# Twenty input panels of a gated decoder block by seven half-size block products, with the mixer branches moved behind them

## The chip, the cores and the metric

The kernel runs on one core of a Trainium2 chip. The metric is the device time of one execution in microseconds (us). 

## The reference, cut to what matters

One layer of a decoder with three parallel token mixers, for 1024 prompt tokens and 64 sample tokens (8 sequences of 8), D = 1024. All 1088 tokens share all weights.

```python
h = rmsnorm(x, norm_g) * (1 + scale) + shift            # scale, shift, gate from silu(c) @ w_mod
(mg, u, va, za, q, k, vb, ob, zb, ig, fg, p, zc) = split(h @ w_in)
va = layernorm(gelu(va));  ya = gelu(u) * chunk_spatial_gate(va) * silu(za)        # branch A
hb = mlstm(q, k, vb, ig, fg, C0, n0, m0)                                           # branch B, chunks of 128
yb = head_layernorm(sigmoid(ob) * hb) * silu(zb)
yc = (multiscale_pool(p) @ w_pool) * pool_scale * silu(zc)                         # branch C
g_a, g_b, g_c = split(sigmoid(mg))
x = x + gate * ((g_a * (ya @ w_br_a) + g_b * (yb @ w_br_b) + g_c * (yc @ w_br_c)) @ w_out)
y = rmsnorm(x, final_norm_g)
```

`h @ w_in` is 1088 x 1024 by 1024 x 13320. All values are fp32; the outputs are y, the new mLSTM states, the pooling rows and the normalised va of the samples.

## The kernel before, in words

**Panels.** Every large product is cut into weight panels of 1024 x 256: 52 of the input projection, 12 of the three branch projections, 4 of the output projection. fp32 is made of two fp32r parts: a high part (a cast on ScalarE, ACT) and a low part (the rest, a subtraction on VectorE, DVE), so each product is three matmuls on TensorE (PE): high by high, high by low, low by high. `Stream` loads a panel in quarters from the SP queue (`raw`) and splits them (L75 the cast, L78 the subtraction), one panel ahead of its use. The activations h stand split in 16 tiles of 128 features by 1088 tokens (`hhi`, `hlo`).

**Two forms of a panel.** `b_panel` (L194) gives [feature, token]: two feature tiles by three token groups of 364, 362 and 362 columns are six *units*, each of 8 x 3 matmuls into one PSUM bank; there are eight banks. After a unit comes its evacuation, some splitting of the next panel, and one `tick`. `a_panel` (L227) gives [token, feature]: nine units of 256 columns. With `kouter` a `b_panel` goes over the eight k tiles outside and holds six banks to its end.

**Side work.** `self.side` is a list of generators; `tick` runs the first one to its next `yield`, so the work of the mixers is strewn between the units in the order of the program. There is no scheduler: each engine executes its instructions in the order in which they are written.

**The order of the program.** `start` makes h and does panels q0, q1, q2; then q3, va (4 `a_panel`), k (4), v (4 `a_panel`), ob (4 `a_panel`), p and zc in turn (8), zb (4), u and za in turn (8), mg (12), the branch projections (12), the output projection (4). Beside k, v and ob run `gen_ln` and `gen_sgu` (branch A: normalise va, mix positions into `sd`), `gen_gates` (rows of the mLSTM gates) and `gen_gate` (the third part of adaLN, tiles `wg`, `wgs`). `gen_pool` (branch C) of a group g starts behind panel p,g. `gen_prompt` and `gen_sample` (branch B) start with zb and run beside zb, u, za and mg, one step a unit.

**The steps of `gen_prompt`**, ten for each chunk of 128 tokens: scores q k (L1179), times the decay E (L1181), split into P (L139, L140); an empty step; two heads, two heads (L1194 with the split state `Cs` and the weighted q `qs`, L1196 with P; evacuated by L1197 to L1199 into t, st and den); k transposed and weighted into `ks` (L1208, L1213, L1214); the state's update for two heads (L1228, evacuated into C by L1230); split of these two into `Cs`, the other two heads, and the start of `lstm_tail` (short operations on `lsm`, a power on GpSimd); split of the other two and the norm of t (L1098); the next chunk's decays (rb, E) and the split of its v into `vs`; `lstm_out` (L1110 transposes t, L1111 makes yb) and the next chunk's qw, split into `qs`. `gen_sample` has some twelve steps of preparation and end, and 32 steps of one sequence and head each: four products with the split state (L1381), two for the update (L1386), the split of the next state, two updates of C (L1391). With each new head eight masked k tiles `km` are made (L1351).

## Time and profile before

| what | value |
|---|---|
| three runs | 1881.25, 1882.26, 1882.21 us; median 1882.21 us |
| profiled execution: span, first to last instruction | 1883.7 us (no other time of it is given) |
| TensorE busy | 1856.6 us, 99% of the span |
| VectorE busy | 871.6 us, 46% |
| ScalarE busy | 555.7 us, 30% |
| GpSimd busy | 212.8 us, 11% |
| matmuls | 12473 |
| bytes moved by DMA | 234.37 MB, 124 GB/s in the mean |

A row of the groups gives line, engine, operation, out<-in by the names of the program, shapes and count, then busy us and mean ns of one, then the engine's idle time just ahead and what ended it. Matmuls overlap, so the time of one in a stream is the length of a stretch of the chain of waits, divided by its matmuls, and not the mean ns of the group. Rows in order of time give start and length in us; idle time ahead stands in square brackets with what ended it.

### The profile page before, as it was taken

What the parts mean: (1) busy time and instruction counts of PE and PEld (TensorE: products, weight loads), DVE (VectorE), ACT (ScalarE), POOL (GpSimd) and SP (SyncE); (2) the same over time, 40 slices, a digit from 0 to 9 for tenths busy, and PEclk for the clock granted to TensorE, in tenths of its full rate; (3) what the DMA queues carried; (4) which work ended last, traced back from release to release, by engine and by line L of the source; (5) the groups of instructions that cost most, each with busy time, mean ns of one, the idle gap of its engine ahead of it and who ended that gap; (6) DMA issues with size and microseconds to landing.
All of it is one profiled execution on the core that took longest, in us unless ns stands there. A gap on an engine that the chain in (4) does not pass through costs nothing.

```text
span 1883.7 us, 30152 instructions
## 1 busy us (share of the span) xinstructions
PE 1856.6 (99%) x12473; PEld 1845.0 (98%) x12473; DVE 871.6 (46%) x1638; ACT 555.7 (30%) x1108; POOL 212.8 (11%) x340
## 2 busy tenths in 40 slices
PE   7999999999999999999999999999999999999998
PEld 7899999999999999999999999999999999999998
DVE  7751125424321445536566666444443324374444
ACT  5352222113332222223333333343222312121223
POOL 3440000011100000000000000021221000000023
PEclk8889999999999999999999999999999999999999
DMA  6233122333432212154353444255555434372422
GB/s 248 96 106 103 41 84 93 99 123 100 151 99 84 65 60 71 59 177 135 118 154 102 148 149 147 82 159 170 184 191 166 172 117 163 108 248 90 153 68 96
DMA packets 155228, 234.37 MB, mean 124 GB/s; under 512 B 16145, under 2 KB 122321, under 8 KB 155091
## 3 DMA queue, kind: packets, MB, share of 16 engines
q1 hardware_dynamic: 137490, 168.33, 28.9%
q0 software_dynamic: 17456, 63.85, 9.4%
q8 instruction: 98, 1.61, 0.3%
q14 instruction: 40, 0.32, 0.1%
q10 hardware_dynamic: 144, 0.26, 0.0%
HBM read 164.10 MB, written 68.30 MB: 123 GB/s over the span
## 4 chain that ended last, share of the span: by engine, by line
PE 94%; DVE 2%; ACT 0%; issue 0%; DMA 0%; POOL 0%; POOLq 0%; SPq 0%; ACTq 0%; DVEq 0%
PE ps L194 63%; PE ps L227 19%; PE ps L233 2%; PE ps L953 1%; PE ps L1228 1%; PE ps L1194 1%; PE ps L456 1%; PE ps L1381 1%; PE ps L1179 1%; PE ps L761 1%; PE ps L1196 1%; PE ps L1110 0%; PE ps L623 0%; PE ps L1386 0%; PE ps L1208 0%
## 5 line engine op out<-in xcount | busy, mean ns | idle before, releaser
L194 PE MATMUL ps<-hhi,whi 128*128 128x362 f32 (+1 forms) x1824 | 602.8, 331 | 0.0
L194 PE MATMUL ps<-hhi,wlo 128*128 128x362 f32 (+1 forms) x1824 | 599.4, 329 | 0.0
L194 PE MATMUL ps<-hlo,whi 128*128 128x362 f32 (+1 forms) x1824 | 599.0, 328 | 0.0
L78 DVE TENSOR_TENSOR wlo<-raw,whi 128x512 fp32r<-128x512 f32 (+1 forms) x272 | 186.2, 700 | 357.3 <-ACT whi L75 357.1
L194 PEld LDWEIGHTS ps<-hhi,whi 128*128 128x128 f32 x1824 | 344.4, 189 | 0.6 <-ACT mg L1028 0.4
L194 PEld LDWEIGHTS ps<-hlo,whi 128*128 128x128 f32 x1824 | 344.7, 189 | 0.0
L194 PEld LDWEIGHTS ps<-hhi,wlo 128*128 128x128 f32 x1824 | 343.6, 188 | 0.0
L227 PE MATMUL ps<-whi,hhi 128*128 128x256 f32 (+1 forms) x768 | 219.3, 286 | 0.0
L227 PE MATMUL ps<-wlo,hhi 128*128 128x256 f32 (+1 forms) x768 | 215.6, 281 | 0.0
L227 PE MATMUL ps<-whi,hlo 128*128 128x256 f32 (+1 forms) x768 | 215.6, 281 | 0.0
L75 ACT CAST whi<-raw 128x512 fp32r<-128x512 f32 (+1 forms) x272 | 161.1, 616 | 108.5 <-PE ps L194 105.4
L194 PE MATMUL ps<-yhi,whi 128*128 128x362 f32 (+1 forms) x576 | 189.3, 329 | 0.0
L194 PE MATMUL ps<-yhi,wlo 128*128 128x362 f32 (+1 forms) x576 | 189.0, 328 | 0.0
L194 PE MATMUL ps<-ylo,whi 128*128 128x362 f32 (+1 forms) x576 | 188.9, 328 | 0.0
L227 PEld LDWEIGHTS ps<-whi,hhi 128*128 128x128 f32 x768 | 144.7, 188 | 0.8
L227 PEld LDWEIGHTS ps<-wlo,hhi 128*128 128x128 f32 x768 | 145.0, 189 | 0.0
L227 PEld LDWEIGHTS ps<-whi,hlo 128*128 128x128 f32 x768 | 144.8, 189 | 0.0
L194 PEld LDWEIGHTS ps<-ylo,whi 128*128 128x128 f32 x576 | 108.5, 188 | 0.0
L194 PEld LDWEIGHTS ps<-yhi,whi 128*128 128x128 f32 x576 | 108.5, 188 | 0.0
L194 PEld LDWEIGHTS ps<-yhi,wlo 128*128 128x128 f32 x576 | 108.3, 188 | 0.0
L227 PE MATMUL ps<-whi,mhl 128*128 128x256 f32 x512 | 91.5, 281 | 0.0
L1028 ACT ACTIVATE mg<-ps 128x362 f32<-128x362 f32 (+1 forms) x72 | 34.1, 473 | 189.0 <-PE ps L194 185.5
(346 smaller groups left out, 2305.3 us busy)
## 6 DMA issues: line engine op xcount, KB each, us to landing
raw<-in_w_in_dram SPq DMA_DIRECT2D x204, 256.0 KB
mgd<-mg POOLq DMA_DIRECT2D x24, 544.0 KB, 3.0
mgr<-mgd SPq DMA_DIRECT2D x24, 544.0 KB
raw<-in_w_br_dram SPq DMA_DIRECT2D x48, 256.0 KB
yraw<-yd SPq DMA_DIRECT2D x16, 544.0 KB
C<-in_state_C_dram SPq DMA_DIRECT2D x32, 256.0 KB
out_dram<-C POOLq DMA_DIRECT2D x32, 256.0 KB, 3.1
ss<-in_w_mod_dram SPq DMA_DIRECT2D x14, 512.0 KB
```

Source lines behind the costliest of these rows:

```text
L75: kb.A.copy(hi, t[:, :, :n])
L78: kb.V.tensor_tensor(out=p["lo"][:, sl, :n], in0=t[:, :, :n], in1=hi.bitcast(F32), op=ALU.subtract)
L194: self.PE.matmul(ps[:, :n], w[:, k, fs], a[:, g0 : g0 + n], start=(k == 0 and j == 0), stop=(k == nk - 1 and j == 2))
L227: self.PE.matmul(p[:, :cols], a[:, ts], w[:, k, :cols], start=(k == 0 and j == 0), stop=(k == KT - 1 and j == 2))
L233: self.PE.matmul(p[:, :cols], stack[:, k, :], w[:, k, :cols], start=(k == 0 and j == 0), stop=(k == KT - 1 and j == 1))
L456: PE.matmul(sums[-1][u][:, :m], w["hi" if ww else "lo"][:, k, fs], a[:, g0 : g0 + m], start=(k == 0 and part == "high" and j == 0), stop=( ...
L761: PE.matmul(p[:, j * 128 : j * 128 + 128], self.va[b * 4 + j][:, fs], self.w_sguT[:, g, :], start=True, stop=True)
L953: self.PE.matmul(p[:, :n], wsl[:, ww, k, fs], a[:, g0 : g0 + n], start=(k == 0 and j == 0), stop=(k == 1 and j == 2))
L1028: A.activation(st[f][:, g0 : g0 + w], ps, AF.Tanh, scale=0.5)
L1179: PE.matmul(p[:, h * 128 : h * 128 + 128], k[:, 2 * h + d, :], q[:, 2 * h + d, :], start=(d == 0), stop=(d == 1))
L1194: PE.matmul(p[:, :258], qs[x][:, 2 * h + d, :], Cs[d][y][:, h, :], start=(d == 0 and j == 0), stop=False)
L1196: PE.matmul(p[:, :258], P[:, x, h, :], vs[y][:, h, :], start=(c == 0 and j == 0), stop=(j == 2))
```

## The change

**Twenty panels by seven products.** The panels of k, zb, zc, u and za are taken as 2 x 2 blocks: the weight panel by halves of its features and of k, and h by halves of k and of the tokens (544 and 544). With sums of blocks on both sides (Strassen's scheme in Winograd's form) seven products give what eight do. Each is 4 k tiles x 3 matmuls for two groups of 272 columns (`HT`). `Stream.step` makes the seven weight blocks with four sums on VectorE and splits each; `gen_factors` makes the sums of h once and splits them, one of them (`put_t4`) over the upper token half of h's first four k tiles, which is kept in `b12d` and loaded back behind the last of the twenty panels. In `seven` six banks are held as three pairs b1, b2, b5. The first product goes to b1 and is copied to b2, where three more are accumulated; b5 takes two; sums between pairs go over SBUF (x12, x22).

**Order.** q, then the twenty (k, zb, zc, then u and za in turn) with no side work, then va, v, ob, p, mg, the branches and the output. `sd` is gone: gelu(u) times silu(za) is stored as `uzd` by the new stage and multiplied in `gen_sgu`; silu(zc) is stored as `zcd` and loaded in `gen_pool`.

**Pace.** The same generators run beside fewer panels: `gen_ln`, `gen_sgu`, `gen_gates` and `gen_gate` beside v and ob with one tick a unit; `gen_pool` beside p with two; `gen_prompt` and `gen_sample` beside mg with three. What is left is drained before p and before the last mg panel. Panel q3 is now accumulated k outside, while the last factors are made.

The core of the diff:

```diff
+        if p["seven"]:
+            b = lambda q: raw[q][:, :512]
+            if j == 1:
+                p["x"] = self.raw("sum")
+            x = None if p["x"] is None else p["x"][:, :512]
+            if j == 1:
+                V.tensor_tensor(out=x, in0=b(1), in1=b(2), op=ALU.add)
+            elif j == 2:
+                V.tensor_tensor(out=x, in0=x, in1=b(0), op=ALU.subtract)
+            elif j == 4:
+                V.tensor_tensor(out=b(1), in0=b(0), in1=b(1), op=ALU.subtract)
+            elif j == 6:
+                V.tensor_tensor(out=x, in0=b(3), in1=x, op=ALU.subtract)
+            src = x if j in (1, 2, 6) else b((0, 0, 0, 3, 1, 2)[j])
+            self.live -= (0, 0, 0, 0, 2, 1, 2)[j]
...
+        hi, lo = (kb.wsp.tile([128, 528], F32R, tag="u", name=kb.nm(x))[:, :n] for x in ("whi", "wlo"))
+        kb.A.copy(hi, src)
+        self.units += 1
+        p["u"].append((hi, lo))
+        self.pending = (lo, src, hi)
+        if not self.defer:
+            self.flush()
...
-            self.tick()
+            self.tick(self.pace)
...
+    ORDER = (1, 5, 6, 2, 7, 4, 3)
...
+        for i, n in enumerate(self.ORDER):
+            st.need(panel, i + 1)
+            wh, wl = panel["u"][i]
+            bank, new = {1: (b1, True), 5: (b5, True), 6: (b2, False), 2: (b1, False), 7: (b2, False), 4: (b2, False),
+                         3: (b5, False)}[n]
+            for g in range(2):
+                gs = slice(g * HT, g * HT + HT)
+                if self.fresh and n == 1:
+                    PE.matmul(b2[:, g, :HT], wh[:, 0:128], B[1][0][0][:, gs], start=True, stop=True)
+                for j in range(4):
+                    bh, bl = B[n][j]
+                    ks = slice(j * 128, j * 128 + 128)
+                    for m, (w, b) in enumerate(((wh, bh), (wh, bl), (wl, bh))):
+                        PE.matmul(bank[:, g, :HT], w[:, ks], b[:, gs], start=(new and j == 0 and m == 0),
+                                  stop=(j == 3 and m == 2), skip_group_check=True)
+                if n == 7:
+                    copy(view(x22)[:, g, :], b2[:, g, :HT])
+            st.units -= 1
+            if n == 1:
+                self.fresh = False
+                A.copy(cut(b2), cut(b1))
+            elif n == 6:
+                copy(view(x12), cut(b2))
+            elif n == 2:
+                evac(0, 0, cut(b1))
+            elif n == 7:
+                add(view(x22), cut(b5))
+                evac(1, 1, view(x22))
+            elif n == 4:
+                evac(1, 0, cut(b2))
+            elif n == 3:
+                add(view(x12), cut(b5))
+                evac(0, 1, view(x12))
+            for _ in range(2):
+                if st.units < st.UNITS and self.ahead(panel, i) < 6:
+                    st.step()
+            self.tick(self.pace)
...
-        for nm_ in ("q", "va", "k", "v", "ob"):
+        for n in range(4):
+            pan["q", n] = st.add(i["w_in"][self.PANEL["q"] + n])
+        for nm_, n in self.SEVEN:
+            pan[nm_, n] = st.add(i["w_in7"][self.PANEL7[nm_] + n], seven=True)
...
-        self.start()
-        self.inputs_of_mixers()
-        self.pool_branch()
-        self.merge_gates()
-        self.finish()
-
+        tc = self.tc
+        with tc.tile_pool(name="psumA", bufs=8, space=PSUM) as self.psum:
+            self.start()
+        with tc.tile_pool(name="pairs", bufs=1, space=PSUM) as self.pairs:
+            self.seven_panels()
+        with tc.tile_pool(name="psumB", bufs=8, space=PSUM) as self.psum:
+            self.inputs_of_mixers()
+            self.pool_branch()
+            self.merge_gates()
+            self.finish()
...
-        self.side = [finish_rows(0), finish_rows(1)]
+        self.st.used(w1)
+        self.st.defer = True
+        self.side = [finish_rows(0), finish_rows(1), self.gen_factors(0), self.gen_factors(1)]
...
+        self.pace = 2
         self.b_panel(self.pan["q", 2], self.h, self.evac_rows(2, self.qd))
+        self.drain()
+        def hook(k):
+            for j in range(2):
+                if k == j + 1:
+                    self.put_t4(j)
+            if k in (1, 3):
+                self.side = [self.gen_factors(2 + k // 2)]
+            self.tick(2)
+            if k in (5, 6):
+                self.put_t4(k - 3)
+        self.b_panel(self.pan["q", 3], self.h, self.evac_rows(3, self.qd), kouter=True, hook=hook)
+        self.drain()
+        self.pace = 1
...
+        V.tensor_tensor(out=a0, in0=a1, in1=a0, op=ALU.subtract)
+        V.tensor_tensor(out=a1, in0=b1, in1=a1, op=ALU.subtract)
+        V.tensor_tensor(out=b1, in0=b1, in1=a0, op=ALU.subtract)
+        V.tensor_tensor(out=b0, in0=b0, in1=b1, op=ALU.subtract)
+        yield
+        t13 = [self.slot([128, T], F32R, name="t13") for _ in range(2)]
+        self.split(a, *t13)
+        if j % 2 == 0:
+            self.t2[j // 2] = [self.slot([128, T], F32R, name="t2") for _ in range(2)]
+        half = slice((j % 2) * W, (j % 2) * W + W)
+        t2 = [t[:, half] for t in self.t2[j // 2]]
+        self.split(b1, *t2)
+        self.t4[j] = b0
+        lo, up = slice(0, W), slice(W, T)
+        both = lambda t, s: tuple(x[:, s] for x in t)
+        self.B[1][j] = both(self.h[j], lo)
+        self.B[2][j] = both(self.h[j + 4], lo)
+        self.B[3][j] = both(self.h[j + 4], up)
+        self.B[4][j] = both(self.h[j], up)
+        self.B[5][j] = both(t13, lo)
+        self.B[6][j] = tuple(t2)
+        self.B[7][j] = both(t13, up)
...
+    def put_t4(self, j):
+        self.split(self.t4.pop(j), *self.B[4][j])
...
+            self.seven(self.pan[nm_, n], self.B, evac, 0.0625 if nm_ == "k" else None)
+        for j in range(4):
+            for m in range(2):
+                S.dma_start(self.h[j][m][:, W:].bitcast(F32), self.b12d[j, m])
...
-        for n in range(4):
-            self.b_panel(self.pan["k", n], self.h, self.evac_rows(n, self.kd, 0.0625))
...
+            uz = self.slot([128, T], name="uz")
+            self.S.dma_start(uz, self.uzd[f])
...
-                    G.dma_start(self.sd[f], s)
+                    V.tensor_tensor(out=s, in0=s, in1=uz, op=ALU.mult)
+                    G.dma_start(self.yd[0][f], s)
...
+        self.pace = 2
...
+                    S.dma_start(gates[f], self.zcd[2 * g + f])
...
-            self.b_panel(self.pan["zc", g], self.h, evac_z)
...
-            self.b_panel(self.pan["zb", n], self.h, evac_zb)
...
-            self.b_panel(self.pan["u", n], self.h, evac_u)
-            self.b_panel(self.pan["za", n], self.h, evac_za)
-
+        self.pace = 3
...
+                self.drain()
+                self.pace = 1
...
-    nc = bacc.Bacc("TRN2", target_bir_lowering=False, num_devices=1)
+    nc = bacc.Bacc("TRN2", target_bir_lowering=False, num_devices=1, dynamic_dma_scratch_size=8192)
```

Two places in the program's order. In the mLSTM's second chunk, TensorE: the scores (qc, kc) and what follows. TensorE before:

```order
L194 MATMUL ps_8367<-hhi_1113,wlo_8078 128x364
L1179 MATMUL ps_8407<-qc_8087,kc_8088 128x128 x8
L194 MATMUL ps_8420<-hhi_931,whi_8077 128x362
L194 MATMUL ps_8420<-hlo_932,whi_8077 128x362
L194 MATMUL ps_8420<-hhi_931,wlo_8078 128x362
L194 MATMUL ps_8420<-hhi_948,whi_8077 128x362
```

and with the change:

```order
L257 MATMUL ps_11535<-hhi_1131,wlo_11121 128x362
L1391 MATMUL ps_11570<-qc_11369,kc_11370 128x128 x8
L1406 MATMUL ps_11586<-Cs_11396,qs_11531 128x258
L1406 MATMUL ps_11586<-Cs_11397,qs_11531 128x258
L1406 MATMUL ps_11586<-Cs_11396,qs_11532 128x258
L1406 MATMUL ps_11586<-Cs_11398,qs_11531 128x258
L1406 MATMUL ps_11586<-Cs_11399,qs_11531 128x258
L1406 MATMUL ps_11586<-Cs_11398,qs_11532 128x258
L1408 MATMUL ps_11586<-vs_11510,P_11580 128x258 x2
L1408 MATMUL ps_11586<-vs_11511,P_11580 128x258
L1406 MATMUL ps_11599<-Cs_11396,qs_11531 128x258
```

Before, the scores have a unit of panel products on both sides, and the heads come two units later. Now the first head (Cs and qs, then vs and P) follows the scores directly; P is made from these scores.

VectorE at the same place, before (zb is the evacuation of the panel beside, wlo a weight split):

```order
L1153 TENSOR_TENSOR qw_8360<-qc_8087,rb_8091 128x4x128 x2
L140 TENSOR_TENSOR qs_8364<-qw_8360,qs_8363 128x1024
L990 SCALAR_TENSOR_TENSOR zb_8392<-zb_8392,ps_8367 128x364
L78 TENSOR_TENSOR wlo_8396<-raw_8085,whi_8395 128x2x256
L78 TENSOR_TENSOR wlo_8396<-raw_8143,whi_8395 128x2x256
L1181 TENSOR_TENSOR E_8309<-ps_8407,E_8309 128x512
L140 TENSOR_TENSOR P_8417<-E_8309,P_8417 128x512
L990 SCALAR_TENSOR_TENSOR zb_8392<-zb_8392,ps_8420 128x362
L78 TENSOR_TENSOR wlo_8396<-raw_8199,whi_8395 128x2x256
L990 SCALAR_TENSOR_TENSOR zb_8392<-zb_8392,ps_8451 128x362
L78 TENSOR_TENSOR wlo_8396<-raw_8399,whi_8395 128x2x256
L1198 SCALAR_TENSOR_TENSOR t_694_8483<-o_8405,ps_8486 128x256
```

and with the change:

```order
L1365 TENSOR_TENSOR qw_11528<-qc_11369,rb_11373 128x4x128 x2
L203 TENSOR_TENSOR qs_11532<-qw_11528,qs_11531 128x1024
L99 TENSOR_TENSOR wlo_11492<-raw_11123,whi_11491 128x512
L1393 TENSOR_TENSOR E_11505<-ps_11570,E_11505 128x512
L203 TENSOR_TENSOR P_11580<-E_11505,P_11580 128x512
L1410 SCALAR_TENSOR_TENSOR t_1470_11583<-o_11568,ps_11586 128x256
L1411 BN_STATS st_1471_11584<-t_1470_11583 128x6
L1410 SCALAR_TENSOR_TENSOR t_1470_11583<-o_11568,ps_11599 128x256
L1411 BN_STATS st_1471_11584<-t_1470_11583 128x6
L1410 SCALAR_TENSOR_TENSOR t_1470_11583<-o_11568,ps_11639 128x256
L1411 BN_STATS st_1471_11584<-t_1470_11583 128x6
L1410 SCALAR_TENSOR_TENSOR t_1470_11583<-o_11568,ps_11652 128x256
```

The evacuations and most weight splits between the steps of the mLSTM are gone: qs, E, P and the four heads' t and st follow each other.

295 lines of the change are left out of this document (186 added, 109 removed).

## The prediction

> **What bounds the kernel now.** I read the page's busy times first, then the chain of waits, then the stretches, then VectorE's instructions in order of time. The page:
>
> ```profile
> span 1883.7 us, 30152 instructions
> PE 1856.6 (99%) x12473; PEld 1845.0 (98%) x12473; DVE 871.6 (46%) x1638; ACT 555.7 (30%) x1108; POOL 212.8 (11%) x340
> ```
>
> TensorE is busy for 99% of the span, so today a shorter stream of products shortens the kernel, and every wait put before a product lengthens it. The chain of waits, by pieces (start us, us, what), gives the price of a product:
>
> ```profile
> 190.61 22.70 PE ps L227 x192
> 1445.09 331.10 PE ps L194 x1992
> ```
>
> 331.10/1992 is 166.2 ns for a product of 362 or 364 columns (362.7 in the mean), 22.70/192 is 118.2 ns for one of 256. A unit of a feature-major panel, 24 products, is 3.99 us. Stretches (us, then busy time and instructions of PE, PEld, DVE, ACT and POOL, granted clock, DMA share, GB/s):
>
> ```profile
> 80.00:100.00 20.00, 17.09 (x87) 15.65 (x86) 15.79 (x20) 5.12 (x11) 8.96 (x5) 0.74 0.08 24
> 885.00:1440.00 555.00, 554.72 (x3594) 552.37 (x3593) 300.83 (x688) 188.90 (x384) 71.25 (x148) 1.00 0.47 147
> 1445.00:1776.00 331.00, 331.00 (x1994) 330.99 (x1993) 146.75 (x219) 69.69 (x102) 3.07 (x5) 1.00 0.44 147
> ```
>
> In 885 to 1440 the mLSTM generators run beside the panels: VectorE works 300.83 us of 555 and TensorE never waits. That slack is what the change spends.
>
> **What the twenty panels gain.** A panel now has 144 products at 166.2 ns, 23.93 us. By seven block products it has 7 x 2 x 4 x 3 = 168 products of 272 columns. No row has 272 columns; the line through the two rows above has 0.45 ns a column, so 125.4 ns, and 168 of them take 21.07 us. 2.86 us by 20 panels is **57.3 us gained** (50 to 60, if the width costs a little more or less).
>
> Beside them VectorE and ScalarE work more: per panel seven halves instead of four to split, four sums of weight blocks, two sums with b5. By the split's row below (700 ns for 512 columns) VectorE has 11 such, 7.7 us, two sums and up to eight evacuation steps of 544 columns at about 0.75 us, 7.5 us: 15.2 of 21.07 us. ScalarE has seven casts and seven or eight copies at about 0.65 us, some 10 us. Each bank pair is written again only after another product of 3.0 us, which covers copy and sum. I take 2 us for all twenty (0 to 15).
>
> **What is paid before and behind them.** The factors: four times (two sums and one split of 1088 columns at 1.29 us, five operations of 544 at about 0.7 us), 7.4 us each, plus four splits, are 32 us of VectorE, in order, under panels q2 and q3 (48 us) that already hold 3 + 4 us of weight splits and waits on ScalarE. The last factors come late for the first panel's second product, and the six banks of q3, now accumulated together, are emptied only at its end: 6 us (2 to 15). The restore of 2.2 MB from `b12d` has the last product (3.0 us) and four tiles of va (96 products, 11.3 us) as cover: 2 us (0 to 6). The adaLN gate: v and ob have 72 ticks, the four generators need more, so `drain` ends the third and fourth part of `gen_gate` with nothing between:
>
> ```profile
> L140 DVE TENSOR_TENSOR wgs<-wg,wgs 128x1024 fp32r<-128x1024 f32 x8 | 9.8, 1226 | 7.6 <-ACT wgs L139 7.6
> L139 ACT CAST wgs<-wg 128x1024 fp32r<-128x1024 f32 x8 | 8.4, 1044 | 0.0
> ```
>
> One cast and two subtractions are 3.5 us before the one product, the rest behind it mostly hidden by ScalarE running ahead: 5 us (2 to 12).
>
> **The pool branch** had two panels of one step per unit for each group; now it has one panel of two steps, and the last group three.
>
> ```profile
> L78 DVE TENSOR_TENSOR wlo<-raw,whi 128x512 fp32r<-128x512 f32 x268 | 183.4, 700 | 352.3 <-ACT whi L75 352.1
> L140 DVE TENSOR_TENSOR plo<-po,phi 128x1088 fp32r<-128x1088 f32 x8 | 10.3, 1292 | 3.0 <-ACT phi L139 2.7
> L923 DVE TENSOR_TENSOR pa<-pb 128x1039 f32<-128x1039 f32 x8 | 9.9, 1234 | 0.0
> L931 DVE SCALAR_TENSOR_TENSOR po<-pa,pb 128x1008 f32<-128x1008 f32 x8 | 9.6, 1201 | 0.0
> L924 DVE TENSOR_TENSOR psa<-psb 128x176 f32<-128x176 f32 x8 | 2.7, 335 | 0.0
> L139 ACT CAST phi<-po 128x1088 fp32r<-128x1088 f32 x8 | 8.8, 1103 | 2.3 <-DVE po L935 2.2
> ```
>
> Per feature tile a level costs 1.23 + 0.33 us, and 1.20 + 1.10 + 1.29 us follow in a chain. Two tiles with one to four levels, and two weight splits between, are 11.7, 14.8, 17.9 and 21.0 us before the group's first product. It comes after three units (12.0 us), for the last group after two (8.0 us). TensorE waits 0 + 2.8 + 5.9 + 13.0 = 22 us (10 to 35).
>
> **The prompt's mLSTM is the large term.** It takes ten ticks for each of eight chunks, now three to a unit, so a chunk has 3.33 units, 13.3 us, and 84 products of its own of up to 258 columns, at 118.2 ns or less 9.9 us: 23.2 us of TensorE. VectorE executes in order; for one chunk, with what ended each idle time in brackets:
>
> ```profile
> 971.75 1.30 DVE L140 TENSOR_TENSOR Cs<-C,Cs 128x516 fp32r<-128x516 f32 x2
> 972.96 1.66 DVE L1230 SCALAR_TENSOR_TENSOR C<-C,decb,ps 128x258 f32<-128x258 f32 x4
> ...
> 976.99 0.16 DVE L152 SCALAR_TENSOR_TENSOR lsm<-lsm 128x4 f32<-128x4 f32 x1 [1.22 <-POOL lsm L149]
> ...
> 977.58 0.16 DVE L1095 TENSOR_TENSOR lsm<-lsm 128x4 f32<-128x4 f32 x1
> ...
> 978.67 1.29 DVE L140 TENSOR_TENSOR Cs<-C,Cs 128x516 fp32r<-128x516 f32 x2
> 979.89 1.38 DVE L1098 TENSOR_SCALAR t<-t,lmv,lsm 128x256 f32<-128x256 f32 x4
> ...
> 982.84 0.68 DVE L1144 TENSOR_TENSOR rb<-rb,c_maskp 128x512 f32<-128x512 f32 x1
> 985.81 1.23 DVE L140 TENSOR_TENSOR vs<-v,vs 128x1032 fp32r<-128x1032 f32 x1 [2.29 <-ACT vs L139]
> ...
> 988.71 1.28 DVE L1111 TENSOR_TENSOR yb<-ps,c_mnorm_gT 128x512 f32<-128x512 f32 x2
> 989.91 1.28 DVE L1153 TENSOR_TENSOR qw<-qc,rb 128x512 f32<-128x512 f32 x2
> 992.37 1.23 DVE L140 TENSOR_TENSOR qs<-qw,qs 128x1024 fp32r<-128x1024 f32 x1 [1.17 <-ACT qs L139]
> ...
> 994.55 0.68 DVE L1181 TENSOR_TENSOR E<-ps,E 128x512 f32<-128x512 f32 x1
> 995.97 0.69 DVE L140 TENSOR_TENSOR P<-E,P 128x512 fp32r<-128x512 f32 x1 [0.73 <-ACT P L139]
> ...
> 999.52 0.42 DVE L1198 SCALAR_TENSOR_TENSOR t<-o,ps 128x256 f32<-128x256 f32 x1 [0.23 <-ACT den L1197]
> ...
> 1001.04 0.43 DVE L1199 BATCH_NORM_STATS2 st<-t 128x6 f32<-128x256 f32 x1
> ```
>
> Stretch by stretch: 971.75 to 977.74 is 5.99 us; Cs and t, 978.67 to 981.27, 2.60; rb to vs 4.20; yb to qs 4.89; E to P 2.11; two heads 1.95, so four 3.9. The chunk's rest stands some 13 us later:
>
> ```profile
> 1013.27 0.48 DVE L1214 SCALAR_TENSOR_TENSOR ks<-ps,cols,ks 128x256 fp32r<-128x256 f32 x1
> ...
> 1015.70 0.48 DVE L1214 SCALAR_TENSOR_TENSOR ks<-ps,cols,ks 128x256 fp32r<-128x256 f32 x1 [0.54 <-ACT ks L1213]
> ...
> 1017.71 1.66 DVE L1230 SCALAR_TENSOR_TENSOR C<-C,decb,ps 128x258 f32<-128x258 f32 x4
> L139 ACT CAST Cs<-C 128x516 fp32r<-128x516 f32 x60 | 35.9, 621 | 0.0
> ```
>
> ks to ks is 2.91, C 1.66, and the cast ahead of the first Cs 0.62. That is 28.9 us; 2.2 weight splits make 30.4 us, of which 7 us are short waits for ScalarE and GpSimd that nothing fills, since the next instruction stands behind. The chain closes on itself: heads need P and qs, the next chunk's transposes need t. So a chunk cannot follow the last in 23.2 us; it needs 30.4, and more, because three ticks stand together: heads 2 and 3 can stand a unit (4 us) behind 0 and 1, and a cast of Cs stands on ScalarE behind the evacuation of the unit ahead. By walking the three alignments of ten ticks to groups of three I get 2 to 6 us of such idling per chunk and take 4: 34.4 us, **11.2 us more than TensorE needs, 78 us for the seven chunks that have a successor**. Bounds: nothing, if ScalarE and GpSimd come early enough to hide their 7 us; 122 us with 8 us at the borders in all eight.
>
> **The sample mLSTM**: 32 steps, three to a unit.
>
> ```profile
> L1391 DVE SCALAR_TENSOR_TENSOR C<-C,decb,ps 128x258 f32<-128x258 f32 x64 | 27.8, 477 | 0.0
> L1351 DVE TENSOR_SCALAR km<-kst,c_bmask 96x256 fp32r<-96x256 f32 x32 | 9.3, 358 | 0.0
> ```
>
> Each step's products need a split state whose subtraction (0.69 us) stands on VectorE behind the last step's two updates (0.87 us). The first of a group also waits for a cast behind the evacuation (about 1.1 us). A group's 18 products, 2.1 us, then take about 4.1 us: 2.0 us by 10.7 groups is 21 us; the four changes of head, eight km each, add some: 25 us (8 to 50; DMA would set the upper end, some 2 MB for 8 us).
>
> **The sum**, against the profiled span of 1883.7 us: -57.3 + 2 + 6 + 2 + 5 + 22 + 78 + 25 = +82.7, so 1966 us. The median of the runs, 1882.21, is 1.5 us under that span: **1965 us**, slower.
>
> **The rivals.**
> 1. *The waits overlap.* TensorE runs ahead, VectorE never idles; its busy time per chunk then is 30.4 - 7 = 23.4 us, even with TensorE's 23.2. With 5 us for the prompt and the lower ends elsewhere (22) the sum is -30: 1852 us, faster. For it: 300.83 of 555 us. Against: the bracketed waits are there while VectorE has time. It decides once a chunk follows in under about 27 us.
> 2. *The clock falls too.* In 80 to 100 us TensorE idled 2.9 of 20 us and was granted 0.74, against 1.00 where it never idles. About 280 us of products stand in the stages where I expect waits; at 0.85 they take 49 us more, half of it on the path: 1990 us. The Trainium skill, "TensorE: Matmul & The Clock Gate", HAM oscillation, says that an idle stretch beyond about one window of 3.4 us halves the clock until it has been busy again; by that rule waits of 4 to 13 us here would each be followed by slow products. This profile's row agrees in direction.
> 3. *The seven products are not bound by TensorE.* If copies, sums and casts, which wait for each other in order, hold a panel at today's 23.9 us, the 57.3 us are not gained: 2022 us. For it: VectorE at 72%. Against: 3.0 us of cover at each step.
> 4. *The same stalls at half their price*, 70 us: 1895 us.
>
> **How the numbers follow.** Forecast 0.58 (its own range 1925 to 2010); rival 1 0.10, rival 2 0.17, rival 3 0.08, rival 4 0.07, of which 0.03 reach no change or faster. Faster by over 0.2% (about what a measurement of this kernel can tell) 0.11, within it 0.02, slower 0.87. 1900 to 2040 leaves out rival 1 and the far tail.
>
> **What would show it.** Right: 272-column products about 125 ns apart and TensorE near 99% in the seven stage, then, in the mg panels, waits of PE for P, qs, t and Cs on VectorE, a chunk every 34 us, VectorE over 80% there, and four mg panels behind it as before. Wrong: a chunk every 25 us with PE at 99%, or waits inside the seven stage.

## The result and the profile after

The kernel became slower, as forecast, but by much more: **2100.81 us** (2095.85 to 2107.09, four runs) against 1882.24 us (1881.25 to 1885.32, four runs), 1.116 times the time before, 95% interval 1.114 to 1.119. The forecast was 1965 us with a range of 1900 to 2040. The loss is 219 us where 83 us were summed up.

The page of the changed kernel, its first rows and TensorE's granted clock in 40 slices:

```profile
span 2105.3 us, 31462 instructions
PE 1900.0 (90%) x12955; PEld 1854.2 (88%) x12955; DVE 1019.9 (48%) x1814; ACT 617.5 (29%) x1202; POOL 220.7 (10%) x356
...
PEclk8999999999999999999998888888889999999999
```

TensorE's share of the span fell from 99% to 90%. It waits about 205 us, and it is even busy for 43 us longer than before, though its products, at the prices of before, add up to some 57 us less. The clock row shows one reason, a stretch of eights from slice 22 to slice 30. Nothing else became busy. VectorE stands at 48%, ScalarE at 29%.

What TensorE waited for, over the whole run (who waits, whom for; us in total, times, longest):

```profile
PE b L353 <- ACT x L330: 36.7, 32, 3.0
PE ps L1322 <- DVE t L1310: 30.4, 8, 5.6
PE ps L257 <- DVE wlo L99: 22.2, 8, 5.3
PE ps L1212 <- ACT phi L202: 17.6, 4, 8.1
PE ps L1593 <- ACT Cs L202: 10.3, 10, 3.5
PE ps L293 <- DVE wlo L99: 8.8, 5, 6.8
...
PE ps L1593 <- DVE Cs L203: 7.6, 15, 2.5
```

The largest row is one that the forecast had priced at 2 us: line 353 issues the block products, and in 32 places they wait for ScalarE to copy an accumulator out. The second is the prompt's transposes behind VectorE's normalised rows, the fourth the pool's product, the fifth and the last the samples' states. These were foreseen. The third is ordinary units that wait for the low part of their own weights, 13.4 us of it in the prompt; the sum had no such wait.

Stretches of the changed kernel: the seven-product stage, the prompt, the samples, and the merge gates left over (us, then busy time and instructions of PE, PEld, DVE, ACT, POOL, granted clock, DMA share, GB/s):

```profile
172.00:659.00 487.00, 445.68 (x3362) 435.94 (x3362) 213.78 (x330) 162.44 (x296) 17.19 (x33) 0.97 0.26 83
1178.00:1470.00 292.00, 235.74 (x1386) 222.91 (x1384) 171.60 (x415) 89.09 (x199) 23.75 (x44) 0.88 0.40 120
1470.00:1592.00 122.00, 95.77 (x514) 87.61 (x514) 72.62 (x165) 39.89 (x76) 38.14 (x86) 0.86 0.55 182
1592.00:1701.00 109.00, 108.32 (x654) 107.57 (x653) 29.06 (x56) 28.52 (x51) 8.00 (x13) 1.00 0.43 142
```

Twenty panels in 487 us are 24.4 us each; an ordinary panel took 23.93 us. **The seven products saved nothing.** In the prompt and the samples TensorE is granted 0.88 and 0.86 of its clock, so its products take longer there as well as wait. The last row is 4.5 panels of uncovered merge gates at full speed, as the forecast said.

Where the 221.6 us between the two spans went, stage by stage. The measured column is the stage's length less what its products take at the prices of the kernel before (from the starts of successive products in the trace); "slow" is the part that is no gap but products further apart than those prices:

| Term of the sum | forecast | measured | of it slow |
|---|---|---|---|
| twenty panels at 125.4 ns a product | -57.3 | -57 | |
| waits inside the seven products | 2 | 66 | 14 |
| transition to the first block product | 6 | 6 | 1 |
| restore, va, v, ob, gates, gate drain | 2 + 5 | 22 | 5 |
| pool | 22 | 30 | 5 |
| prompt | 78 | 98 | 32 |
| samples | 25 | 46 | 13 |
| merge gates left, and all behind | 0 | 10 | 0 |

### The profile page after: what moved, and what is told of

Read it like the earlier page. It is cut to its first block, busy times and chain, and to the rows that moved or that the text cites. A ratio compares the mean times of both kernels' runs of the same rounds, so it can differ in the third digit from the quotient of the medians.

```text
span 2105.3 us, 31462 instructions
## 1 busy us (share of the span) xinstructions
PE 1900.0 (90%) x12955; PEld 1854.2 (88%) x12955; DVE 1019.9 (48%) x1814; ACT 617.5 (29%) x1202; POOL 220.7 (10%) x356
## 5 line engine op out<-in xcount | busy, mean ns | idle before, releaser
L257 PE MATMUL ps<-hhi,wlo 128*128 128x362 f32 (+1 forms) x864 | 292.0, 338 | 16.5 <-DVE wlo L99 16.5
L257 PE MATMUL ps<-hhi,whi 128*128 128x362 f32 (+1 forms) x864 | 294.0, 340 | 0.0
L257 PE MATMUL ps<-hlo,whi 128*128 128x362 f32 (+1 forms) x864 | 291.1, 337 | 0.0
L353 PE MATMUL b<-t,whi 128*128 128x272 f32 x960 | 190.0, 295 | 31.1 <-ACT x L330 29.1
L353 PE MATMUL b<-hhi,whi 128*128 128x272 f32 x640 | 189.5, 296 | 9.5 <-ACT x L330 7.6
L353 PE MATMUL b<-hlo,whi 128*128 128x272 f32 x640 | 187.4, 293 | 0.0
L353 PE MATMUL b<-hhi,wlo 128*128 128x272 f32 x640 | 186.8, 292 | 0.0
L257 PEld LDWEIGHTS ps<-hhi,wlo 128*128 128x128 f32 x864 | 169.5, 196 | 17.7 <-DVE wlo L99 17.7
L257 PEld LDWEIGHTS ps<-hhi,whi 128*128 128x128 f32 x864 | 170.9, 198 | 0.5 <-PE ps L1527 0.4
L257 PEld LDWEIGHTS ps<-hlo,whi 128*128 128x128 f32 x864 | 170.1, 197 | 0.0
```

Of the source, the lines that this page charges most:

```text
L257: self.PE.matmul(ps[:, :n], part(panel, w, k, fs), a[:, g0 : g0 + n], start=(k == 0 and j == 0), stop=(k == nk - 1 and j == 2))
L353: PE.matmul(bank[:, g, :HT], w[:, ks], b[:, gs], start=(new and j == 0 and m == 0), stop=(j == 3 and m == 2), skip_group_check=True)
```

## The experiments

The lines in the diffs are those of the changed kernel or of the kernel that an experiment starts from. Each is timed beside the kernel before.

### 1. The same order with eight products

Is it the seven products that cost, or the order that they force on the rest? The twenty panels are ordinary ones again, in the same place, with every mixer still behind them:

```diff
-            pan[nm_, n] = st.add(i["w_in7"][self.PANEL7[nm_] + n], seven=True)
+            pan[nm_, n] = st.add(i["w_in"][self.PANEL[nm_] + n])
...
-            self.seven_panels()
+            self.eight_panels()
...
-        self.side = [finish_rows(0), finish_rows(1), self.gen_factors(0), self.gen_factors(1)]
+        self.side = [finish_rows(0), finish_rows(1)]
...
+            self.b_panel(self.pan[nm_, n], self.h, evac)
```

(`eight_panels` is the loop over the twenty panels with the same evacuations; the factors, their copy to `b12d` and the products of q3 for all units at once fall away with the seven products.)

> The twenty panels of k, zb, zc, u and za as ordinary panels of 144 products, at the same place, ahead of the mixers; no factors, q3 ordinary again; all else as in the change. Theory: in the change the stage of the twenty panels takes 483 us, 24.1 us a panel, which is what ordinary panels take (23.9), so the seven products gain nothing and the whole loss comes from the mixers beside fewer panels: 2085 to 2105 us, twenty panels in 478 to 482 us, the prompt's mLSTM still some 36 us a chunk. Rival: the seven products do gain about 57 us and the later stages cost that much more than they seem to: 2140 to 2165 us.

Measured: 2084.55 us (2083.77 to 2085.32), 1.108 times before (1.105 to 1.111), half a microsecond under the theory's range. With ordinary products in the same order the kernel is 16 us *faster* than with seven, and 203 us slower than before. Chunks of the prompt started 32.9, 30.6, 34.5, 44.5, 30.9, 35.2 and 42.2 us apart, as in the changed kernel (32.7, 32.8, 34.8, 45.1, 31.2, 35.2, 42.1). So the price of the order is some 200 us, and beside it the block products, which should have paid 57 us back, cost 16.

### 2. The wait inside the seven products

What the block products wait for is seen best in one panel of zb. ScalarE in order of time (start us, duration, engine, line, operation, in brackets the idle time before it and what ended it):

```profile
280.51 0.62 ACT L130 CAST whi<-sum 128x512 fp32r<-128x512 f32 x1 [2.12 <-DVE sum L119]
281.04 0.38 ACT L330 COPY x<-b 128x272 f32<-128x272 f32 x1
283.39 0.39 ACT L330 COPY x<-b 128x272 f32<-128x272 f32 x1 [1.98 <-PE b L353]
```

and TensorE's two idle places at the same time:

```profile
281.47 0.52 PE L353 MATMUL b<-t,whi 128*128 128x272 f32 x2 [2.23 <-ACT x L330]
...
283.83 0.60 PE L353 MATMUL b<-hhi,whi 128*128 128x272 f32 x1 [0.48 <-ACT x L330]
```

Product 7 lies in two banks of the pair b2, one for each half of the tokens. Behind its first half ScalarE copies that half out (line 330), but ScalarE is in the cast of a weight block, and that cast waited 2.12 us for VectorE's sum of blocks. Until the copy at 281.04 is over, the second half of product 7 does not start, though it writes the other bank: the wait is for the tile, which is the pair (the first kernel below tests this). When the second half is done, product 4 writes the same pair straight away and waits for its copy again. Products 7, 7 and 4 write b2 with nothing between them; each other pair does have another product between.

Two kernels take this away by different means. The first makes b2 two tiles, one for each half, so that only a half's own copy is waited for:

```diff
-        self.b2 = self.pairs.tile([128, 2, 512], F32, tag="b2", name="b2")
+        self.b2 = [self.pairs.tile([128, 512], F32, tag=f"b2{g}", name=f"b2{g}") for g in range(2)]
```

(Copies and evacuations of b2 are then two instructions, one for each half.)

> The change with the pair b2 as two tiles, one for each column group; order and work are the same but that copies and evacuations of b2 are two instructions of 272 columns. Theory: the second half of product 7 and the first half of product 4 wait because ScalarE's copy of one half is held against the other half of the pair as well; with two tiles the 0.77 us waits go and the 2.5 us waits shrink to about 1 us: the stage falls from 483 to 435 to 455 us, the kernel to 2050 to 2075 us. Rival: the waits come from ScalarE being late behind casts that wait for the weight sums; then the stage stays above 470 us.

Measured: 2057.08 us (2055.84 to 2058.32), 1.093 times before (1.090 to 1.096).

The second keeps the pair, gives product 3 a pair of its own, and lays product 3 between 7 and 4; x22 is then copied once for both halves:

```diff
-    ORDER = (1, 5, 6, 2, 7, 4, 3)
+    ORDER = (1, 5, 6, 2, 7, 3, 4)
...
+        b3 = self.pairs.tile([128, 2, 512], F32, tag="b3", name=self.nm("b3"))
...
-                         3: (b5, False)}[n]
+                         3: (b3, True)}[n]
...
-                if n == 7:
-                    copy(view(x22)[:, g, :], b2[:, g, :HT])
...
             elif n == 7:
+                copy(view(x22), cut(b2))
+                add(view(x12), cut(b5))
                 add(view(x22), cut(b5))
```

(The weight blocks are made in the new order, too.)

> The change with product 3 in a pair of its own (b3, the two free banks), done between products 7 and 4, and one copy of b2 behind product 7: a product of 3.0 us now stands between the copy of b2 and the next write to it, as between all other pairs; VectorE has one sum of 544 columns more per panel. Theory: the 51 us of gaps in the stage go nearly all, and the 13 us of slow products behind them: the stage takes 422 to 432 us, the kernel 2040 to 2055 us. Rival (late ScalarE, or VectorE at its limit): gaps move to the next product and the stage stays above 450 us.

Measured: 2054.13 us (2050.96 to 2057.3), 1.092 times before (1.087 to 1.096). The same stretch, of the kernel with two tiles and then of the one with its own pair for product 3:

```profile
174.00:611.00 437.00, 426.54 (x3361) 423.88 (x3360) 212.74 (x340) 168.14 (x354) 16.39 (x32) 1.00 0.28 92
```

```profile
174.00:611.00 437.00, 426.80 (x3362) 425.93 (x3362) 228.59 (x352) 161.53 (x283) 17.32 (x33) 0.99 0.29 93
```

The stage lasts 437 us in both, 50 less than in the changed kernel, and the remaining waits for copies are, in the first and in the second kernel:

```profile
PE b L353 <- ACT x L330: 10.2, 11, 1.5
```

```profile
PE b L354 <- ACT b L359: 7.0, 3, 2.4
```

The first are those of product 4 for its own half, the second those of product 6 for the copy from b1 to b2. Both kernels fall in the range of their theory, though the stage of the second was expected to take 422 to 432 us.

426.80/3362 is 126.9 ns for a product of 272 columns where the forecast took 125.4, and 437/20 is 21.8 us a panel where it took 21.07: the price of the block products was right, and the wait was what hid it. Against the same order with eight products (2084.55 us) the second kernel gains 30 us: 42 in this stage, where twenty ordinary panels of 23.93 us take 479, less what stands around it. With the gaps the clock came back too, from 0.97 to 0.99 and 1.00; of the 14 us of slow products in this stage 4 are left. The one with its own pair for product 3 is the base of the runs that follow, 2054 us.

### 3. Two steps behind a unit, not three

The mixers' steps follow a unit of 24 products three at a time. With two for the pool's last group and the prompt there is more dense work beside each chunk:

```diff
-        self.side += [self.gen_prompt(), self.gen_sample()]
-        self.pace = 3
+        self.side += [self.gen_prompt(), self.faster(), self.gen_sample()]
+        self.pace = 2
```

`faster` sets the pace to 3 once the prompt is done. The kernel is otherwise the changed one.

> The change with two ticks a unit beside the mg panels until the prompt's mLSTM is done, then three. A chunk has five units instead of 3.33, so TensorE alone needs 29.5 us a chunk. Theory: a chunk is held by VectorE's chain of 30 us and the idling at group borders, so a chunk follows in 32 to 36 us as before, and 1.67 units a chunk, 53 us, of the panels behind are done in that time: 2035 to 2060 us. Rival: each group has its own price and more groups cost more; a chunk takes 40 us or more and the kernel stays within 15 us of the change's 2101 us.

Measured: 2072.21 us (2070.78 to 2073.64), 1.101 times before (1.098 to 1.105): 29 us won of the changed kernel's loss. Chunks were 38.7, 37.4, 40.0, 40.7, 38.1, 38.8 and 43.2 us apart, so neither theory held: more dense products, less idle time (48 us in the prompt against 66), but chunks 3 us *longer*. The chunk did not keep its length, as the theory had it, and the kernel did not stay where it was, as the rival had it. The next guess is that each *group* of steps has a price.

### 4. Where a step stands, and what stands ahead of it

One reason for a group to cost is ScalarE's order. In the kernel with its own pair for product 3, ScalarE's largest wait beside the prompt is its evacuation of the merge gates, for the end of a unit:

```profile
ACT mg L1239 <- PE ps L257: 69.5, 19, 13.0
ACT den L1410 <- PE ps L1409: 29.7, 31, 1.8
```

While it waits, the casts and exponentials behind it wait as well. Issued behind the steps, the evacuation blocks nothing:

```diff
+            if self.late:
+                self.tick(self.pace)
             evac(f, g, p[:, : GROUPS[g][1]])
             self.prep_some(panel, u, len(units))
-            self.tick(self.pace)
+            if not self.late:
+                self.tick(self.pace)
```

(`prep_some`, the splitting of the next panel, moves behind the steps with it.)

> Base: the kernel with product 3 in its own pair (2054 us; its seven prompt chunks 35.8 us apart on average, prompt stage 288.6 us long of which TensorE idles 68.8 us). One edit, for the merge-gate panels alone: ScalarE's evacuation (tanh) of a unit is issued behind the three steps that follow the unit, no longer ahead of them. Theory A (ScalarE takes its work in order, and the evacuation, which waits for the end of the unit, holds up casts and exponentials of the mixers that could already run): chunks 31 to 33 us apart, prompt stage 255 to 270 us, 2020 to 2040 us. Theory B (the delay lies inside a group of three steps, from TensorE to VectorE and ScalarE and back, and nothing of it can start earlier): chunks within 1 us of 35.8, 2045 to 2060 us.

Measured: 2027.68 us (2021.74 to 2028.08), 1.076 times before (1.073 to 1.079), 26 us less than the base. But the samples gave 18 us of it (121.5 to 103.4 us) and the prompt only 8 (288.6 to 280.2 us, chunks 34.9 us apart where theory A had 31 to 33). What stood ahead of the steps is a cause for the samples; for the prompt it is a small part. How much of it is the evacuation and how much the weight splits, which were moved with it, no run separates.

The other reason is that three steps follow each other on TensorE with nothing between. The next kernel lays them inside the unit:

```diff
             for k in range(nk):
                 mms(p, f, g, k)
+                if self.spread and k in (2, 5) and self.nps - n0 <= 3:
+                    self.tick()
+                    left -= 1
             evac(f, g, p[:, : GROUPS[g][1]])
             self.prep_some(panel, u, len(units))
-            self.tick(self.pace)
+            self.tick(left)
```

(`left` counts the steps still due for this unit; `nps - n0` is the number of accumulators taken since its start.)

> Same base (2054 us). For the merge-gate panels, the three steps of the mLSTM that followed each unit of 24 products back to back are laid inside the unit: one after 9 products, one after 18, one behind the unit (a second inner step is put behind the unit where it would need more than the free accumulators). Same instructions, same number of steps per unit. Theory B (a step waits for VectorE and ScalarE work that the step just ahead of it set off, and no dense product lies between): TensorE's idle time of the prompt stage falls from 68.8 us to under 30, the sample's from 34 to under 15, slow products with it; 1995 to 2030 us. Rival (each step waits for its own work, wherever it stands): idle time within 15 us of 103 for both stages, 2040 to 2060 us.

Measured: 2015.14 us (2014.8 to 2016.56), 1.070 times before (1.068 to 1.073), 39 us less than the base and inside theory B's range, though not by its numbers: the idle time of the prompt went from 69 to 53 us only (it said under 30), that of the samples from 34 to 18. Chunks were 32.9 us apart.

Then two steps per unit, one after half of the products and one behind, from the pool on:

```diff
-                if self.spread and k in (2, 5) and self.nps - n0 <= 3:
+                if self.spread and k == 3 and self.nps - n0 <= 3:
...
-        self.pace = 3
+        self.pace = 2
```

(`spread` is set at the start of the pool branch, too.)

> Same base (2054 us), and from the pool panels on two steps per unit, one in the middle of the unit (after 12 of 24 products) and one behind it, so that some 2 us of dense products lie between any two steps; the pool, prompt and sample steps then last about as long as the dense units do. Theory B (idle time comes from steps that follow one another): pool stage idle from 24.5 us to under 10, prompt and sample together from 103 to under 35, slow products of the three stages from 46 to under 20; 1945 to 1990 us. Rival (a step has its price wherever it stands, as the kernel with two steps back to back suggested): idle time over 90 us in the three stages, 2030 to 2060 us.

Measured: 1972.42 us (1969.95 to 1972.55), 1.047 times before (1.045 to 1.049), 82 us less than the base and inside theory B's range. Chunks are 33.7 us apart, 5.9 us less than with two steps back to back (39.6 us), although just as many dense products lie beside each. The pool's idle time fell only from 24.5 to 19 us, where under 10 was expected. The stretch of the prompt:

```profile
1136.00:1413.00 277.00, 257.26 (x1698) 248.65 (x1697) 176.53 (x424) 96.28 (x220) 26.45 (x49) 0.99 0.47 144
```

TensorE is busy for 93% of it, where it was 81% in the changed kernel, at a clock of 0.99. With the evacuation, and again the weight splits, behind the step at the unit's end as well:

```diff
+            if self.spread:
+                self.tick(left)
+                left = 0
             evac(f, g, p[:, : GROUPS[g][1]])
             self.prep_some(panel, u, len(units))
             self.tick(left)
```

> As the kernel with two steps spread over each unit (1972 us), and ScalarE's evacuation of the unit is issued behind the step at its end, as in the run with the evacuation behind the steps. Theory A and B are separate causes: together 1952 to 1964 us, the idle time of the prompt stage from 24 us to 15 to 19 and of the sample stage from 14 us to 7 to 10. Rival (with the steps apart, ScalarE has caught up by the time an evacuation blocks it): 1966 to 1978 us.

Measured: 1957.81 us (1955.86 to 1959.21), 1.039 times before (1.037 to 1.041), in the range of two separate causes. Idle time fell by 5 us in the pool, 2.5 in the prompt (to 21, where 15 to 19 was expected) and 3 in the samples.

### 5. The clock

In the stages with gaps TensorE was granted 0.86 to 0.88. Two kernels put products of zeros into the longest of the prompt's waits, ahead of the transposes that end a chunk (29.7 us in all there):

```diff
             p = self.ps()
+            if j == 0 and m == 128:
+                for _ in range(56):
+                    PE.matmul(p[:64, :64], self.zero, self.zero, start=True, stop=True)
```

> Same base (2054 us). Ahead of the eight transposes that end a prompt chunk, where TensorE waits 3 to 5.6 us for VectorE's normalised rows (29.7 us in all over 7 of 8 chunks), 56 products of 64x64 zeros into the accumulator that the transposes then overwrite: 59 ns each, 3.3 us a chunk. They replace idle time and compute nothing. Theory (the granted clock falls because of these gaps): slow products in the prompt stage cost under 15 us instead of 25.9, and the kernel takes 2040 to 2049 us. Rival (the clock follows something else, such as the whole share of busy time in the stage): slow products 22 to 30 us, 2050 to 2060 us.

Measured: 2057.58 us (2056.09 to 2058.51), 1.093 times before (1.091 to 1.095). The filler took 6.75 us a chunk, twice what was planned, since each product stands as two rows of 60 ns:

```profile
1224.82 6.75 PE L1322 MATMUL ps<-zero 128*64 128x64 f32 x112
```

so it was run once more with `range(28)`:

> As the kernel with 56 filler products, with 28 of them ahead of the transposes. There, each 64x64 product of 4-byte numbers stood as two rows of 60 ns in the trace, so 56 took 6.75 us a chunk, where the wait was 4.2 us on average: the filler itself then made some 2.5 us a chunk longer, 20 us in all, though the kernel lost only 3.5 us. 28 take 3.4 us and fit the wait. Theory (the granted clock falls because of these gaps): merge-gate products beside the prompt back near 328 ns from 337 to 347 ns, and the kernel takes 2038 to 2048 us against 2054 us. Rival (what the clock gives back is no more than the filler costs, or the first filler run differed for another reason): 2050 to 2060 us.

Measured: 2059.44 us (2058.38 to 2060.63), 1.094 times before (1.091 to 1.096). The stretch of the prompt in the base, with 28 and with 56 products:

```profile
1131.00:1418.00 287.00, 228.01 (x1376) 214.70 (x1375) 171.26 (x415) 87.70 (x197) 23.77 (x44) 0.90 0.40 121
```

```profile
1131.00:1418.00 287.00, 246.99 (x1798) 232.33 (x1798) 170.85 (x414) 85.46 (x190) 23.76 (x44) 0.92 0.38 117
```

```profile
1131.00:1418.00 287.00, 263.81 (x2272) 253.03 (x2271) 171.61 (x415) 88.17 (x197) 23.79 (x44) 0.97 0.39 120
```

The clock did follow the gaps: 0.90, 0.92, 0.97. The dense products beside the prompt sped up with it, from 347 to 339 and 332 ns each in the trace for the first of each three with 362 columns. But no time was gained: chunks stand 35.8, 36.0 and 35.9 us apart on average. What the transposes still waited for t, in the base and with 28 products:

```profile
PE ps L1323 <- DVE t L1311: 29.7, 7, 5.6
```

```profile
PE ps L1326 <- DVE t L1311: 6.3, 5, 2.2
```

With 56 products this wait is gone: the filler takes 6.75 us where the wait was 4.2, so it makes the transposes some 2.5 us late in each chunk, and yet the chunks are no longer than before. Something gave these 2.5 us back; the faster clock may have, but no run separates it. With 28 products the filler fits into the wait in most chunks, but the clock rose by 0.02 only, and nothing was gained. So the gaps set the clock, and filling them with zeros does not pay. How much of what the clock takes in this stage lies on the path that sets the end stays open.

### 6. The mixers alone

Does a chunk have a length of its own, whatever TensorE has to do beside it? All steps of the prompt and the samples run before the first merge-gate panel, with no dense product among them:

```diff
         self.pace = 3
+        self.drain()
```

> Base: the kernel with product 3 in its own pair (2054 us, chunks 35.8 us apart with 3 units, 11.8 us, of merge-gate products in each). All steps of the prompt and the samples run before the first merge-gate panel, one behind the other, with no dense product among them; the merge gates follow uncovered. Nothing is left out. Theory (a chunk is a chain through ScalarE, VectorE and TensorE of 28 to 34 us, whatever TensorE is given beside it, so that time below that is only idle time of TensorE): chunks 28 to 34 us apart; the merge gates then cost 11 panels of 24 us by themselves; 2090 to 2140 us. Rival (a chunk is the sum of its units and of waits that its steps have each; without the units it shrinks by their 11.8 us): chunks 22 to 26 us apart, 2045 to 2085 us.

Measured: 2149.04 us (2148.93 to 2149.33), 1.142 times before (1.139 to 1.144), 9 us above the theory's range and far from the rival's. The first, second, third and last of the eight chunks by the products that start them:

```profile
1117.14 1.95 PE L1393 MATMUL ps<-qc,kc 128*128 128x128 f32 x16
1142.24 2.86 PE L1393 MATMUL ps<-qc,kc 128*128 128x128 f32 x16
1173.65 2.52 PE L1393 MATMUL ps<-qc,kc 128*128 128x128 f32 x16
...
1328.17 3.62 PE L1393 MATMUL ps<-qc,kc 128*128 128x128 f32 x16
```

(1328.17 - 1142.24)/6 is **31.0 us a chunk, with nothing beside it**. The base has 36.3 us by the same six, (1382.39 - 1164.53)/6, with three or four units of merge gates in a chunk: 80 products on average, 13.3 us at 166.2 ns (the expectation's 11.8 us are three units). So 13 us of dense work lengthen a chunk by 5.3 us: a chunk is a chain of some 31 us through the three engines, and most of TensorE's dense work falls into its holes. The stretch of these chunks (columns as above):

```profile
1117.00:1356.00 239.00, 135.71 (x713) 120.31 (x712) 158.18 (x393) 65.94 (x147) 17.23 (x34) 0.74 0.36 103
```

and, of the same stretch, what TensorE waited for:

```profile
PE ps L1324 <- DVE t L1312: 65.9, 8, 8.7
PE ps L1408 <- ACT qs L202: 24.6, 7, 4.3
```

VectorE, the busiest, works 66% of the stretch; no engine bounds it. The chain does: the transposes wait for t (65.9 us), the first heads for qs (24.6 us). VectorE stands in the middle of it. In the six chunks behind the first it works 123.03 us, 20.5 each, and waits 10.1 us each for ScalarE and GpSimd, most of all here:

```profile
1142.24:1328.17 185.93, 106.41 (x553) 94.47 (x553) 123.03 (x300) 51.94 (x115) 12.37 (x24) 0.72 0.36 102
```

```profile
DVE t L1412 <- ACT den L1411: 19.9, 24, 1.1
DVE vs L203 <- ACT vs L202: 13.8, 6, 2.3
```

The 31 us hold at a granted clock of 0.72; how long the chain would be at the full clock was not tried.

### 7. Twelve panels by seven products

If cover is what is missing, more of it should pay although it costs products. Here k, zb and zc alone go by seven products; u and za are ordinary panels again, ahead of the merge gates, with branch A's product in their evacuation as in the kernel before. That is 138 units of dense work for the mixers' steps, so four steps on three units:

```diff
-Builder.SEVEN = tuple((b, n) for b in ("k", "zb", "zc") for n in range(4)) + tuple(
-    (b, n) for n in range(4) for b in ("u", "za"))
+Builder.SEVEN = tuple((b, n) for b in ("k", "zb", "zc") for n in range(4))
...
+            if self.spread:
+                self.count += 1
+                left = 2 if self.count % 3 == 0 else 1
...
+            self.b_panel(self.pan["u", n], self.h, evac_u)
+            self.b_panel(self.pan["za", n], self.h, evac_za)
```

> As the last, with seven products for the twelve panels of k, zb and zc alone; the eight panels of u and za are ordinary ones again, ahead of the merge gates, with branch A's product formed in their evacuation as in the kernel before. That gives 138 units of dense products beside the mixers instead of 90, so four steps on three units. Theory (what the mixers cost is set by the dense products they have for cover): idle and slow time of the pool, prompt and sample stages together from about 77 us to under 25, against 8 times 2.1 us that seven products would have saved on u and za: 1915 to 1942 us. Rival (those stages' waits stand in chains that more cover does not break): 1960 to 1990 us.

Measured: 1936.93 us (1934.92 to 1937.32), 1.028 times before (1.026 to 1.030), in the theory's range. Eight panels by eight products instead of seven, with the steps thinned out over them, made the kernel 21 us *faster*. The stretches of the seven products, the pool and the prompt:

```profile
174.00:431.00 257.00, 255.60 (x2018) 255.38 (x2018) 133.88 (x209) 93.74 (x164) 12.84 (x25) 0.99 0.33 107
780.00:975.00 195.00, 192.83 (x1157) 192.53 (x1156) 97.30 (x161) 46.48 (x92) 16.52 (x42) 0.99 0.37 118
985.00:1339.00 354.00, 337.65 (x2187) 335.73 (x2186) 207.11 (x483) 123.93 (x260) 29.99 (x54) 0.97 0.42 131
```

The block products now run as they were meant to, 257/12 or 21.4 us a panel, and the pool stage has lost its idle time. It is still 54 us slower than the kernel before. The idle and slow time of pool, prompt and samples was 44 us, not under 25, and outside them some 36 us remain that the kernel before does not have: 6 ahead of the block products, 22 beside va, v and ob and in the gate's drain, 8 at the end. 12 panels save some 30 us. No combination that was run beats the kernel before.

## Why the forecast was right in sign and wrong in size

**What bounds the kernel, and the price of a block product: right.** 125.4 ns from a line through two other widths; 126.9 ns measured in the stage without most of its waits. With these waits gone the stage took 437 us, where twenty ordinary panels take 479, so 42 of the 57 us were reached.

**The step that failed first** is the sentence "Each bank pair is written again only after another product of 3.0 us, which covers copy and sum", with its 2 us (0 to 15). It holds for b1 and b5, not for b2: in the order 1, 5, 6, 2, 7, 4, 3 the two halves of product 7 and product 4 follow one another in b2, and the wait is for the pair and not for the half. The stage lost 66 us and not 2, and a change of a few lines took 50 of them away. Two things in the diff could have shown it: the `copy` inside the loop over the halves, which reads a pair that the next pass of the loop writes, and the table of pairs read in the order of `ORDER` rather than by product. The 3.0 us of cover were also no cover against ScalarE's own order: the copy stood behind a cast that had to wait 2.12 us for VectorE. Rival 3 gave this outcome, a panel held at 23.9 us, a chance of 0.08 and a price of 57 us; it came true by way of waits and not of VectorE's load.

**The prompt: the mechanism right, the size 20 us short.** The chain of VectorE's instructions gave 30.4 us a chunk; alone it runs at 31.0. That they are so near is in part luck: the forecast put the chain together from 23.4 us of VectorE's work and 7 of its waits, and alone it has 20.5 and 10.1 (1.5 of the 23.4 are weight splits, which the chain alone does not hold). The 4 us added for the alignment of ten steps to groups of three were 5.3: (1432.05 - 1178.13)/7 is 36.3 us by the first and the last of these rows of the changed kernel.

```profile
1178.13 1.95 PE L1391 MATMUL ps<-qc,kc 128*128 128x128 f32 x16
...
1432.05 1.95 PE L1391 MATMUL ps<-qc,kc 128*128 128x128 f32 x16
```

TensorE's own need is 24.2 us of that by the products of the trace, where the forecast had 23.2, so the seven chunks lose 84 us, 6 more than forecast. The other 14 are the eighth chunk, which the sum let go free since it has no successor: it waits as the others do. One wait had no term: the low part of a merge-gate panel's weights stands on VectorE behind the mixers' instructions, and three times between 1178 and 1470 us a unit waits for it.

```profile
PE ps L257 <- DVE wlo L99: 13.4, 3, 5.3
```

The first of these splits starts at 1253.64, behind qs and P, which had themselves waited for ScalarE. "VectorE over 80% there" was wrong: 171.60 of 292 us are 59%. A chain through in-order engines can set the pace with none of them near its limit.

**The samples: 46 us for 25.** The mechanism, states split late behind the last step's updates and the unit's evacuation, was right: L1593 waits for Cs on ScalarE and VectorE. The sum had 1.1 us by 10.7 groups, 12 us, for the evacuation; moving it and the weight splits was worth 18. Slow products, which this term left out, are 13 us.

**The gates and the drain: 22 us for 7.** The step to va took 1.3 us (2 forecast for the restore), though VectorE's last block sum and not the restored rows ended that wait; the drain took 6.4 (5 forecast). What was counted at nothing was branch A's layer norm. It used to stand beside the k panels, whose units last 4 us; now it stands beside v, whose units last 2.8 us, and VectorE falls behind. In order of time on VectorE:

```profile
815.27 1.22 DVE L998 TENSOR_TENSOR va<-va,lng 128x1024 f32<-128x1024 f32 x1
816.53 1.23 DVE L999 TENSOR_TENSOR va<-va,lnb 128x1024 f32<-128x1024 f32 x1
817.68 0.68 DVE L99 TENSOR_TENSOR wlo<-raw,whi 128x512 fp32r<-128x512 f32 x1
```

and TensorE, for the low parts of that weight block:

```profile
818.41 0.58 PE L293 MATMUL ps<-wlo,hhi 128*128 128x256 f32 x1 [6.81 <-DVE wlo L99]
```

That the shorter units are the cause is read from the trace; no run tried it. The 8 us of waits for weight splits in the last stage, which had none in the kernel before, are not explained.

**The pool: 30 us for 22**, the same mechanism, inside its bounds. **Transition: 6 for 6.**

**The clock (rival 2): it happened, and its price was read wrongly.** About 70 us of the table are products further apart than before. The rival took half of such time to be on the path. In the seven-product stage it was: gaps and slow products went together. In the prompt the fillers gained no time, but they do not show how much of it lies on the path. The Trainium skill, "TensorE: Matmul & The Clock Gate", has a section on frequent short idling (A second HAM failure mode: psum-queue depth-cycling) beside the rule of one idle window of 3.4 us that the forecast cited: it lets the clock swing between full and half speed by frequent gaps that are each short. The seven-product stage agrees with that section, with 32 waits of at most 3.0 us, 1.1 on average, one of 5.0 us at its start, and a granted clock of 0.97. That mean is made of full and of half clock, as around the waits that end at 281.47 and 283.83 us, shown above:

```profile
283.00:286.40 3.40, 2.92 (x13) 2.59 (x13) 1.87 (x3) 1.55 (x3) 0.00 (x0) 0.50 0.00 0
286.40:306.90 20.50, 18.44 (x147) 18.22 (x145) 9.27 (x15) 6.70 (x12) 1.07 (x2) 1.00 0.32 106
306.90:310.30 3.40, 3.09 (x12) 2.77 (x12) 0.00 (x0) 0.22 (x2) 0.00 (x0) 0.50 0.00 0
```

So the forecast erred where it took a stage from its parts' loads and sizes (a cover of 3 us, VectorE at 72%) instead of walking through the order in which each engine meets its instructions. Where it did walk, in the prompt, it came within 2 us a chunk.

## What to carry to other kernels

A cheaper product in a kernel at 99% of TensorE pays only if the work that ran beside the dear one still has somewhere to run: 57 us of products saved here took away the cover of the mixers, whose prompt and samples then last 414 us with TensorE busy for 80% of them, and making eight of the panels dear again, with the steps thinned out over them, gained 21 us. Before counting on a buffer being free, write down the tile that each instruction writes in program order and look for the same tile twice in a row. And where a stage is a chain through engines that each work in order, measure the chain alone first (31 us here): taking all dense work away did not bring it below that, but its steps can be spread so that something dense lies between them, and that gained 82 us, part of it in the pool and the samples.

## What the runs showed of the hardware

- The waits in the program are for the tile as it is named, not for the bank: with both halves of b2 in one tile, the second half waited for the copy of the first (36.7 us in 32 waits, with those of product 4); with a tile per half 10.2 us were left, in 11 waits, all of product 4.
- The mean granted clock falls with TensorE's idle time, as a mixture of stretches at 0.50 and at 1.00 (283.0 to 310.3 us of the changed kernel): 0.99 with 98% busy (seven products with a pair for product 3), 0.97 with 92% (the changed kernel's), 0.88 with 81% (its prompt), 0.74 with 57% (the mixers alone). It is not the share alone: with the steps spread, 93% had 0.99.
- A 64x64 product of 4-byte zeros is two rows of 60 ns in the trace, 120 ns in all.
